# State-space heads: forward product and sum as one scalar_tensor_tensor per token tile

## The chip, the cores and the metric

The kernel runs on one core of one Trainium2 chip. The metric is the time of the program on the device in microseconds (us); less is better. The engines of the core run at once, each through its own queue in order: TensorE (PE for matmuls, PEld for the load of their stationary operand), VectorE (DVE), ScalarE (ACT), GpSimd (POOL) and SyncE (SP), which here only issues DMA transfers. They wait for each other by semaphores.

## The reference, cut to what matters

One inference step of a model of two layers, on 128 context tokens and 512 latent ones, all in fp32. Each layer has three branches read from one input projection, differential attention, a gated MLP, and a bidirectional state-space mixer with 16 heads. The mixer is the branch concerned:

```python
dt = jax.nn.softplus(dt_raw.reshape(bt, T, 2, M_HEADS).astype(F32) + dt_bias.astype(F32))
for d in range(2):                       # forward, backward
    dt_d = dt[:, :, d]
    y_d, fin = ssd_scan(_orient(xh * dt_d[..., None], d), _orient(dt_d * A[d], d),
                        _orient(bh, d), _orient(ch, d), init_states[:, d])
    ys.append(_orient(y_d, d) + d_skip[d].astype(F32)[:, None] * xh)
y = (ys[0] + ys[1]).reshape(bt, T, M_INNER)

# inside ssd_scan, chunks of 128 tokens:
a_cs = jnp.cumsum(a, -1)
decay_in = jnp.exp(segsum(a))
cb = jnp.einsum("bclhn,bcshn->bchls", c, b)
y_diag = jnp.einsum("bchls,bcshp->bclhp", cb * decay_in, xdt)
```

So inside each chunk a head needs a 128 x 128 matrix for each direction, c b^T under a triangular mask, times the step size dt of the source token and the decay between two tokens; it is multiplied with the head's values.

## The kernel before

**Data.** The 640 tokens are five tiles of 128. Weights stream from HBM in chunks of 128 x 1024. Every large matmul is done three times with operands split into a rounded high part and a rest: `w_hi` (L414, ScalarE) casts a chunk to its high part, `w_lo` (L423, VectorE) subtracts it to get the low part. `dense_F` (L535 to L537) then issues 24 matmuls per half of 320 tokens; one unit is 48 matmuls.

**Order.** One program order is written out by generators: TensorE's dense units are the clock (`tick`, after every six matmuls), and small tasks (`go`, with `yield n` for a pause of n ticks) put their instructions between. So the place of each instruction in its engine's queue is fixed when the program is built. Memory too is planned there: `Plan.place` runs the program once with nothing behind it, and lays each block (`al`, freed by `fr`) by first fit.

**The state-space stage.** For each pair of heads f (0 to 7 in the first layer; numbered on as 8 to 15 in the second) the units `xbc` and `z` run, after some of them (f = 3, 5, 7) also one of the gate projections `mga`. `ssd_pair` (L1334 to L1424) does what both heads share: the transposes of the values (L1343, copied by ScalarE at L1346), two products on GpSimd (L1354), the chunk states (matmuls L1365, recurrence L1373 on VectorE, copy of the final state L1376 on ScalarE, its store L1378 on the SP queue, copies L1382 and L1383), the output matmuls (L1394 with the head matrices M, L1396 with the states), their evacuation L1406, and the gate (L1412) and the sum of squares (L1420 on ScalarE, L1422) with products on GpSimd. Other tasks run between: the depthwise convolution (L1190 to L1194 copies, L1208 and L1214 on ScalarE, L1210, L1211 and L1216 on VectorE) and the gate of z (L1060 on ScalarE, L1062 on VectorE), and L1641, an evacuation with tanh on ScalarE.

**One head.** `ssd_head` (L1426) makes M for one head, 640 columns (five chunks of 128). `gf` and `gb` are c b^T under the two masks, shared by eight heads; `dt` has the step sizes, 32 columns (16 heads, two directions) for each of five tiles; `e[0]` and `e[1]` get the cumulated decay rows by DMA (L1437) and their bias by ScalarE (L1446, five instructions of 128 columns per direction). VectorE multiplies gf and gb by dt (L1443, once for each direction, two ticks apart), adds the two products (L1449), takes the smaller of the two exponents (L1451); ScalarE exponentiates (L1454), VectorE scales the states' operand (L1455) and forms M (L1457). The first head of a pair starts 5 ticks after its loads were issued and the second 12 (`D_HEAD`), so their instructions interleave.

Of the kernel before, what the change touches and what calls it, by code (L numbers as in the profile page):

```python
# [10 lines left out]
ALU = mybir.AluOpType  # L11
# [3 lines left out]
NT = 5  # L15
# [218 lines left out]
class Build:  # L234
# [1191 lines left out]
    def ssd_head(self, S, hh):  # L1426

        nc = self.nc
        f, l = S["f"], S["l"]
        h = 2 * f + hh  # L1430
        yield from self.until(lambda: f // 4 in self.G)
        gf, gb, cd = self.G[f // 4]
        e = [self.al(640) for _ in range(2)]
        ec = self.al(512)
        for d in range(2):
            j = 16 * d + h
            nc.sync.dma_start(out=self.v(e[d]), in_=self.csd[l][j:j + 1, :].to_broadcast([128, 640]))  # L1437
            nc.sync.dma_start(out=self.v(ec, 0, 512, 64 * d, 64 * d + 64), in_=self.ecd[l][j:j + 1, :].to_broadcast([64, 512]))
        yield D_HEAD[hh]
        d3 = self.v(self.dt).rearrange("p (c j) -> p c j", c=5)  # L1440
        w = [self.al(640) for _ in range(2)]
        for d, gg in enumerate((gf, gb)):
            nc.vector.tensor_tensor(out=self.v(w[d]).rearrange("p (c n) -> p c n", c=5), in0=self.v(gg).rearrange("p (c n) -> p c n", c=5),  # L1443
                                    in1=d3[:, :, 16 * d + h:16 * d + h + 1].to_broadcast([128, 5, 128]), op=ALU.mult)
            for c in range(NT):
                nc.scalar.activation(self.v(e[d], 128 * c, 128), self.v(e[d], 128 * c, 128), AF.Identity,  # L1446
                                     bias=self.v(self.cs, 32 * c + 16 * d + h, 1))
            yield 2
        nc.vector.tensor_tensor(out=self.v(w[0]), in0=self.v(w[0]), in1=self.v(w[1]), op=ALU.add)  # L1449

        nc.vector.tensor_tensor(out=self.v(e[0]), in0=self.v(e[0]), in1=self.v(e[1]), op=ALU.min)  # L1451
        self.fr(e[1], w[1])
        yield 2
        nc.scalar.activation(self.v(e[0]), self.v(e[0]), AF.Exp)  # L1454
        nc.vector.tensor_tensor(out=self.v(ec), in0=self.v(cd), in1=self.v(ec), op=ALU.mult)  # L1455
        yield 2
        nc.vector.tensor_tensor(out=self.v(e[0]), in0=self.v(e[0]), in1=self.v(w[0]), op=ALU.mult)  # L1457
        self.fr(w[0])
        S["M", hh], S["C", hh] = e[0], ec

    def ssd_end(self, l):
# [423 lines left out]
```

## Time and profile before

| | |
|---|---|
| time, median of 3 runs | 2187.92 us (2187.67 to 2189.08) |
| the profiled execution: time | 2191.47 us |
| its span (first to last instruction) | 2189.3 us |
| granted TensorE clock, mean | 0.996 |
| busy: PE, DVE, ACT, POOL | 98%, 66%, 47%, 8% |
| L1443, VectorE, 64 instructions | 0.81 us at least, 2.19 at most |
| L1449, VectorE, 32 instructions | 0.81 us at least, 1.94 at most |

The time of an execution is the span and about 2 us around it. Times inside the trace count from the start of the span. A line Lnnn is a line of the kernel before, also where the engine's work was issued by a helper. "Busy" of PE is not speed: matmuls are pipelined, and one of 320 columns is counted with 0.31 us while the next starts 0.14 us after it.

### The profile page before, as it was taken

How to read it: one execution, taken by the hardware profiler on the slowest of the kernel's cores; microseconds unless marked ns; L12 is line 12 of the kernel's file. 1: busy time of each engine (PE TensorE's matmuls, PEld its weight loads, DVE VectorE, ACT ScalarE, POOL GpSimd, SP SyncE). 2: the span in 40 equal slices, each digit the busy share in tenths (PEclk: the TensorE clock that was granted, in tenths of full speed). 3: DMA queues.
4: the chain of work that ended last, by engine and by line, in shares of the span. 5: the costliest groups of instructions: out<-in, count | busy, mean ns of one | idle time of the engine just before them, and what ended most of it. 6: DMA issues, size and time to landing. Idle time of an engine off the chain costs nothing.

```text
span 2189.3 us, 38380 instructions
## 1 busy us (share of the span) xinstructions
PE 2155.2 (98%) x15288; PEld 2090.4 (95%) x15288; DVE 1439.2 (66%) x2688; ACT 1032.8 (47%) x2240; POOL 184.0 (8%) x185
## 2 busy tenths in 40 slices
PE   7999999999999999999989999999999999999998
PEld 4999999999999999999879999999999999999996
DVE  5577677568556679976475777774464532799754
ACT  3566566532333257762265656563323322677521
POOL 0000000000101113320000000000001001132100
PEclk9999999999999999999999999999999999999999
DMA  7433333234224455633134333321222231555331
GB/s 295 123 102 99 90 102 104 85 120 145 77 78 147 166 153 155 165 95 135 68 121 119 100 91 101 110 77 63 94 77 69 78 119 41 141 155 147 117 125 49
DMA packets 94859, 246.17 MB, mean 112 GB/s; under 512 B 13940, under 2 KB 27348, under 8 KB 94680
## 3 DMA queue, kind: packets, MB, share of 16 engines
q1 hardware_dynamic: 94680, 243.72, 35.8%
q8 instruction: 120, 1.97, 0.4%
q14 instruction: 59, 0.48, 0.1%
HBM read 208.75 MB, written 8.70 MB: 99 GB/s over the span
## 4 chain that ended last, share of the span: by engine, by line
PE 88%; DVE 5%; ACT 3%; DMA 2%; issue 2%; SPq 0%; DVEq 0%; ACTq 0%
PE psum L536 19%; PE psum L537 19%; PE psum L535 18%; PE psum L477 6%; PE psum L476 6%; PE psum L478 6%; PE psum L964 4%; PE psum L1011 3%; PE psum L994 2%; DMA plain<-csd 1%; PE psum L1133 1%; DVE plain L1451 1%; DMA plain<-in_wp_dram 1%; PE psum L1394 1%; ACT rounded L414 1%
## 5 line engine op out<-in xcount | busy, mean ns | idle before, releaser
L536 PE MATMUL psum<-shared,rounded 128*128 128x320 f32 x3136 | 969.2, 309 | 0.0
L535 PE MATMUL psum<-shared,rounded 128*128 128x320 f32 x3136 | 967.0, 308 | 0.0
L537 PE MATMUL psum<-shared,rounded 128*128 128x320 f32 x3136 | 962.1, 307 | 0.0
L535 PEld LDWEIGHTS psum<-shared,rounded 128*128 128x128 f32 x3136 | 589.4, 188 | 4.5 <-issue 3.8
L537 PEld LDWEIGHTS psum<-shared,rounded 128*128 128x128 f32 x3136 | 589.3, 188 | 0.0
L536 PEld LDWEIGHTS psum<-shared,rounded 128*128 128x128 f32 x3136 | 587.8, 187 | 0.1
L423 DVE TENSOR_TENSOR rounded<-plain,rounded 128x1024 fp32r<-128x1024 f32 (+2 forms) x226 | 279.9, 1239 | 166.0 <-ACT rounded L414 159.7
L414 ACT CAST rounded<-plain 128x1024 fp32r<-128x1024 f32 (+2 forms) x226 | 235.3, 1042 | 188.7 <-PE psum L536 160.4
L476 PE MATMUL psum<-rounded,shared 128*128 128x256 f32 (+2 forms) x920 | 296.3, 322 | 0.0
L477 PE MATMUL psum<-rounded,shared 128*128 128x256 f32 (+2 forms) x920 | 292.2, 318 | 0.0
L478 PE MATMUL psum<-rounded,shared 128*128 128x256 f32 (+2 forms) x920 | 290.8, 316 | 0.9 <-DVE shared L850 0.9
L478 PEld LDWEIGHTS psum<-rounded,shared 128*128 128x128 f32 x920 | 173.7, 189 | 11.0 <-DVE shared L850 1.3
L476 PEld LDWEIGHTS psum<-rounded,shared 128*128 128x128 f32 x920 | 173.8, 189 | 8.7
L477 PEld LDWEIGHTS psum<-rounded,shared 128*128 128x128 f32 x920 | 173.7, 189 | 8.3 <-DVE rounded L423 0.2
L972 DVE TENSOR_REDUCE plain<-psum 128x1 f32<-128x640 f32 (+1 forms) x160 | 107.9, 714 | 88.0 <-PE psum L964 84.7
L978 ACT ACTIVATE plain<-psum,plain 128x640 f32<-128x640 f32 (+1 forms) x160 | 112.1, 709 | 4.5 <-DVE plain L972 3.0
L1641 ACT ACTIVATE plain<-psum 128x320 f32<-128x320 f32 x96 | 41.7, 437 | 129.8 <-PE psum L537 118.6
L964 PE MATMUL psum<-shared 128*128 128x320 f32 (+1 forms) x576 | 100.0, 312 | 0.1
L1707 POOL TENSOR_SCALAR plain<-plain 128x1024 f32<-128x1024 f32 x2 | 5.6, 2778 | 1003.9 <-DMA plain<-in_bs_dram 537.6
L1017 ACT ACTIVATE plain<-psum,plain 128x128 f32<-128x128 f32 x80 | 29.4, 368 | 124.3 <-PE psum L1011 85.3
L964 PEld LDWEIGHTS psum<-shared 128*128 128x128 f32 x576 | 84.6, 189 | 1.3 <-ACT plain L978 1.0
L1073 ACT ACTIVATE plain<-psum 128x320 f32<-128x320 f32 (+1 forms) x62 | 27.7, 447 | 121.0 <-PE psum L537 60.8
(277 smaller groups left out, 2687.6 us busy)
## 6 DMA issues: line engine op xcount, KB each, us to landing
plain<-in_wp_dram SPq DMA_DIRECT2D x252, 512.0 KB, 4.0
shared<-in_wp_dram SPq DMA_DIRECT2D x40, 512.0 KB, 7.2
shared<-csd SPq DMA_DIRECT2D x36, 320.0 KB, 5.8
shared<-shared SPq DMA_DIRECT2D x64, 160.0 KB, 3.0
plain<-csd SPq DMA_DIRECT2D x28, 320.0 KB, 5.3
plain<-plain SPq DMA_DIRECT2D x128, 64.0 KB, 2.0
plain<-in_wp_dram SPq DMA_DIRECT2D x12, 528.0 KB, 4.2
shared<-shared SPq DMA_DIRECT2D x32, 192.0 KB, 2.6
```

What stands on the lines that cost most here:

```text
L414: self.nc.scalar.copy(self.r(blk[0], 0, sz), self.v(self.w_raw[i], 0, sz))
L423: self.nc.vector.tensor_tensor(out=self.r(blk[1], 0, sz), in0=self.v(raw, 0, sz), in1=self.v(blk[0], 0, sz), op=ALU.subtract)
L476: mm(out, ht, wh, start=(k == 0), stop=False)
L477: mm(out, ht, wl, start=False, stop=False)
L478: mm(out, lt, wh, start=False, stop=(k == KD - 1))
L535: mm(out, wh, xh, start=(k == 0), stop=False)
L536: mm(out, wh, xl, start=False, stop=False)
L537: mm(out, wl, xh, start=False, stop=(k == KD - 1))
L964: mm(self.P[:, ss[m] + half, 0:n], self.r(H["q"], 1280 * i + 640 * m + 128 * t, 128), k, start=(i == 0), stop=(i == 1))
L972: nc.vector.tensor_reduce(out=self.v(st, m, 1), in_=src[m], op=ALU.max, axis=AX.XY if t else AX.X, negate=True)
L978: nc.scalar.activation(pv, src[m], AF.Exp, bias=self.v(st, m, 1), accum_out=self.v(st, 2 + m, 1))
L1011: mm(out, self.v(wt, 128 * j, 128), self.v(H["vg"], 256 * j + 256, 128) if j < 4 else self.v(H["cv"]), start=(j == 0), stop=(j == 4))
```

## The change

For each head the product of gf with the forward step sizes is no longer formed by itself. The backward product w = gb * dt stays one instruction and moves to the place where the forward one stood. At the place of the sum stand five instructions `scalar_tensor_tensor`, one for each token tile, w = gf * dt + w, where dt is a column of one number per partition. One block of 640 columns less is held per head, and the planner lays out the blocks anew.

```diff
         yield D_HEAD[hh]
         d3 = self.v(self.dt).rearrange("p (c j) -> p c j", c=5)
-        w = [self.al(640) for _ in range(2)]
-        for d, gg in enumerate((gf, gb)):
-            nc.vector.tensor_tensor(out=self.v(w[d]).rearrange("p (c n) -> p c n", c=5), in0=self.v(gg).rearrange("p (c n) -> p c n", c=5),
-                                    in1=d3[:, :, 16 * d + h:16 * d + h + 1].to_broadcast([128, 5, 128]), op=ALU.mult)
+        w = self.al(640)
+        nc.vector.tensor_tensor(out=self.v(w).rearrange("p (c n) -> p c n", c=5), in0=self.v(gb).rearrange("p (c n) -> p c n", c=5),
+                                in1=d3[:, :, 16 + h:17 + h].to_broadcast([128, 5, 128]), op=ALU.mult)
+        for d in range(2):
             for c in range(NT):
                 nc.scalar.activation(self.v(e[d], 128 * c, 128), self.v(e[d], 128 * c, 128), AF.Identity,
                                      bias=self.v(self.cs, 32 * c + 16 * d + h, 1))
             yield 2
-        nc.vector.tensor_tensor(out=self.v(w[0]), in0=self.v(w[0]), in1=self.v(w[1]), op=ALU.add)
+        for c in range(NT):
+            nc.vector.scalar_tensor_tensor(out=self.v(w, 128 * c, 128), in0=self.v(gf, 128 * c, 128), scalar=self.v(self.dt, 32 * c + h, 1),
+                                           in1=self.v(w, 128 * c, 128), op0=ALU.mult, op1=ALU.add)
 
         nc.vector.tensor_tensor(out=self.v(e[0]), in0=self.v(e[0]), in1=self.v(e[1]), op=ALU.min)
-        self.fr(e[1], w[1])
+        self.fr(e[1])
```

Below these lines w[0] is w. The changed kernel is two lines longer there: its L1442 is the backward product, L1450 the five new instructions, and its L1453, L1457 and L1459 are L1451, L1455 and L1457 of before.

On VectorE, in the first layer, at the pairs 2 and 3, before:

```order
879 L1406 SCALAR_TENSOR_TENSOR plain<-plain,psum 128x128
880 L1406 SCALAR_TENSOR_TENSOR plain<-plain,psum 128x512
881 L1449 TENSOR_TENSOR shared_7166<-shared_7166 128x640
882 L1451 TENSOR_TENSOR plain<-plain,shared_7166 128x640
883 L1455 TENSOR_TENSOR plain<-plain 128x512
884 L1062 SCALAR_TENSOR_TENSOR plain<-plain,psum 128x320
885 L1443 TENSOR_TENSOR shared_7166<-plain 128x640
886 L1457 TENSOR_TENSOR plain<-plain,shared_7166 128x640
887 L1443 TENSOR_TENSOR plain<-plain 128x640
888 L423 TENSOR_TENSOR rounded<-shared_7166,rounded 128x1024
889 L1373 SCALAR_TENSOR_TENSOR plain<-plain,psum 128x64 x6
890 L1449 TENSOR_TENSOR shared_7166<-shared_7166,plain 128x640
```

The first L1449 belongs to the first head of the pair, the two L1443 and the last L1449 to the second. At the same place in the changed kernel:

```order
876 L1406 SCALAR_TENSOR_TENSOR plain<-plain,psum 128x128
877 L1406 SCALAR_TENSOR_TENSOR plain<-plain,psum 128x512
878 L1450 SCALAR_TENSOR_TENSOR shared_7166<-plain,shared_7166 128x128 x5
879 L1453 TENSOR_TENSOR plain<-plain,shared_7166 128x640
880 L1457 TENSOR_TENSOR plain<-plain 128x512
881 L1062 SCALAR_TENSOR_TENSOR plain<-plain,psum 128x320
882 L1442 TENSOR_TENSOR shared_7166<-plain 128x640
883 L1459 TENSOR_TENSOR plain<-plain,shared_7166 128x640
884 L423 TENSOR_TENSOR rounded<-shared_7166,rounded 128x1024
885 L1373 SCALAR_TENSOR_TENSOR shared_7166<-shared_7166,plain,psum 128x64 x6
886 L1450 SCALAR_TENSOR_TENSOR shared_7166<-plain,shared_7166 128x128 x5
```

One L1443 of the two is gone, from between L1457 and L423, and each L1449 has become five instructions. On TensorE, ScalarE, GpSimd and the SP queue the instructions stand in the same order as before, only some tiles lie elsewhere.

## Rows read from the trace of the kernel before

**Rows 1.** The page, busy time, share of the span, instructions

```profile
PE 2155.2 (98%) x15288; PEld 2090.4 (95%) x15288; DVE 1439.2 (66%) x2688; ACT 1032.8 (47%) x2240; POOL 184.0 (8%) x185
```

**Rows 2.** Busy time by stage, 797 to 962 and 1876 to 2041 together

```profile
sum 330.00, PE 326.66 PEld 312.57 DVE 312.47 ACT 243.78 POOL 106.72; mean PE 163.33 PEld 156.29 DVE 156.23 ACT 121.89 POOL 53.36
```

**Rows 3.** Who waited for L1457: us in total, times

```profile
  PEld psum L1394: 5.8, 12
```

**Rows 4.** The chain of waits, pair 4 to 5: start, us, what

```profile
894.15 0.28 ACT plain L1376
894.44 0.34 SPq L1378
894.88 4.37 DMA shared<-csd
899.27 1.57 ACT shared L1446 x5
```

**Rows 5.** VectorE in order of time, pair 3: start, us, instruction, idle before

```profile
855.70 1.55 DVE L1443 TENSOR_TENSOR shared<-plain 128x640 f32<-128x640 f32 x2
...
858.13 1.23 DVE L423 TENSOR_TENSOR rounded<-shared,rounded 128x1024 fp32r<-128x1024 f32 x1 [0.48 <-ACT rounded L414]
859.27 1.00 DVE L1406 SCALAR_TENSOR_TENSOR plain<-plain,psum 128x128 f32<-128x128 f32 x2
860.19 0.82 DVE L1449 TENSOR_TENSOR shared<-shared 128x640 f32<-128x640 f32 x1
860.92 1.89 DVE L1451 TENSOR_TENSOR plain<-plain,shared 128x640 f32<-128x640 f32 x1
862.74 1.75 DVE L1455 TENSOR_TENSOR plain<-plain 128x512 f32<-128x512 f32 x1
864.41 0.47 DVE L1062 SCALAR_TENSOR_TENSOR plain<-plain,psum 128x320 f32<-128x320 f32 x1
864.81 1.54 DVE L1443 TENSOR_TENSOR shared<-plain 128x640 f32<-128x640 f32 x1
...
867.81 1.23 DVE L423 TENSOR_TENSOR rounded<-shared,rounded 128x1024 fp32r<-128x1024 f32 x1
```

**Rows 6.** GpSimd in order of time, pair 3

```profile
860.30 3.64 POOL L1354 TENSOR_TENSOR plain<-shared,plain 128x640 f32<-128x640 f32 x2 [9.80 <-ACT shared L1346]
863.90 1.76 POOL L1412 TENSOR_TENSOR plain<-plain 128x640 f32<-128x640 f32 x1
```

**Rows 7.** ScalarE in order of time, pair 3

```profile
862.85 0.74 ACT L1454 ACTIVATE plain<-plain 128x640 f32<-128x640 f32 x1 [2.36 <-DVE plain L1451]
863.49 3.02 ACT L1446 ACTIVATE shared<-shared,plain 128x128 f32<-128x128 f32 x10
...
866.74 1.04 ACT L414 CAST rounded<-shared 128x1024 fp32r<-128x1024 f32 x1
```

**Rows 8.** VectorE in order of time, attention end of the first layer

```profile
729.39 1.22 DVE L706 SCALAR_TENSOR_TENSOR plain<-plain 128x1024 f32<-128x1024 f32 x1
...
730.54 1.90 DVE L706 SCALAR_TENSOR_TENSOR plain<-plain 128x1024 f32<-128x1024 f32 x1
```

**Rows 9.** GpSimd at the same time

```profile
729.56 1.79 POOL L1165 TENSOR_TENSOR plain<-plain 128x320 f32<-128x320 f32 x1 [2.37 <-DVE plain L1162]
```

**Rows 10.** Groups by line and shape: count, busy us, mean ns

```profile
L820 DVE SCALAR_TENSOR_TENSOR shared<-plain,shared 128x128 fp32r<-128x128 f32 x8 | 2.8, 347 | 0.0
```

**Rows 11.** VectorE in order of time, pair 1

```profile
825.06 2.19 DVE L1457 TENSOR_TENSOR plain<-plain,shared 128x640 f32<-128x640 f32 x1
```

**Rows 12.** ScalarE in order of time, pair 4

```profile
880.15 0.44 ACT L1060 ACTIVATE plain<-psum 128x320 f32<-128x320 f32 x1 [0.67 <-PE psum L537]
```

**Rows 13.** VectorE in order of time, pair 4

```profile
882.94 1.94 DVE L1449 TENSOR_TENSOR shared<-shared 128x640 f32<-128x640 f32 x1
```

**Rows 14.** GpSimd in order of time, pair 4

```profile
882.25 1.95 POOL L1422 TENSOR_TENSOR plain<-plain,shared 128x640 f32<-128x640 f32 x1 [2.18 <-ACT shared L1420]
884.28 1.73 POOL L1354 TENSOR_TENSOR shared<-shared,plain 128x640 f32<-128x640 f32 x1
```

More of the change, by code (lines that the diff above doesn't have):

```diff
@@ L1456, in ssd_head @@
         yield 2
-        nc.vector.tensor_tensor(out=self.v(e[0]), in0=self.v(e[0]), in1=self.v(w[0]), op=ALU.mult)
-        self.fr(w[0])
+        nc.vector.tensor_tensor(out=self.v(e[0]), in0=self.v(e[0]), in1=self.v(w), op=ALU.mult)
+        self.fr(w)
         S["M", hh], S["C", hh] = e[0], ec
```

## The prediction

> **What bounds the kernel now.** The page comes first: TensorE is busy for 98% of the span, VectorE for 66% [rows 1]. A share over the whole span says little about an edit of one stage, so the second view is the table of stages. The state-space heads run in two stretches, one in each layer, at 797 to 962 and 1876 to 2041 us. In these 330 us TensorE is busy for 326.7 and VectorE for 312.5, which is 95%, with ScalarE at 74% [rows 2]. So both engines are nearly full there, and the question is which waits for which. The third view, who waited for line 1457, answers it: the matmuls of line 1394, which read the finished head matrix M, held their weight loads for it 12 times, 5.8 us together [rows 3]. The two stretches hold 16 pairs of heads; TensorE arrives a little before M in most of them. Nothing is to spare on the way to M.
>
> The fourth view, the chain of waits, shows that way closing on itself. DVE's L1373 of one pair releases L1376 on ScalarE, that the store L1378 on the SP queue; the loads of the next pair's decay rows (L1437) stand behind it in that queue, land 4.37 us later, and release ScalarE's L1446 [rows 4]. From there it goes through the weight split (L414 on ScalarE, L423 on VectorE) to L1449, L1451, the exponential L1454, ten L1446, the next L414 and L423, and to the next L1373. In pair 3 one sees each link [rows 5 to 7]: the first L423 starts at 858.13, L1451 begins at 860.92 and lasts 1.89, L1454 starts at 862.85 right behind it, ten L1446 and an evacuation follow, L414 starts at 866.74, and L423 at 867.81, where VectorE has just become free as well. A delay of L1451 is a delay of everything behind it, since ScalarE takes its instructions in order.
>
> **Why L1451 lasts 1.89 us.** The median of such an instruction, two SBUF operands of 640 columns, is 0.82; L1449 just before it shows that length [rows 5]. The difference is GpSimd. Its two products of L1354 start at 860.30 and are followed by L1412 at 863.90 [rows 6], and three VectorE instructions are long there: L1451 with 1.89, L1455 with 1.75, L1443 with 1.54. Each ends about 0.7 us after a GpSimd product does. L1062, which reads PSUM, starts inside the third product and takes 0.47 [rows 5]. So VectorE instructions with two SBUF operands and GpSimd products take turns, one instruction at a time, and a turn costs VectorE about 1.13 us: in pair 4 the product begun at 884.28 could not run until L1449 ended (882.94 + 1.94 = 884.88), and was over at 884.28 + 1.73 = 886.01 [rows 13, 14]. Scalar_tensor_tensor obeys as well: of two L706 back to back, a product of GpSimd that arrived in the first is let in before the second, which takes 1.90 instead of 1.22 [rows 8, 9].
>
> **The change part by part.** Per head, two instructions of 640 columns go: the forward product (L1443) and the sum (L1449). Five scalar_tensor_tensor of 128 columns come in the place of the sum; the backward product moves up to the place of the forward one. TensorE, ScalarE, GpSimd and the SP queue keep their order. Over 32 heads, 64 instructions go and 160 come.
>
> *Busy time of VectorE.* Neighbours overlap: two L1443 take 1.55 together [rows 5], so each occupies 1.55 - 0.82 = 0.73, and two that go free 1.47 us per head. The same form as the new one lasts 0.347 for 128 columns [rows 10]; with the same overlap of 0.09 it occupies 0.26, and five take 1.30. So VectorE is relieved by 0.17 us a head, 5.4 us in all. But the two halves lie in different places. The product that goes frees 0.73 before an L423 which waits for ScalarE anyway (in pair 3 VectorE idles 0.48 before the one at 858.13 [rows 5]), or before the second L423, where ScalarE's L414 is just as late (866.74 + 1.04 = 867.78 against 867.81 [rows 5, 7]). What hides the loss hides the gain: I count it as nothing. The sum that becomes five costs 1.30 - 0.73 = 0.57 more, in front of L1451, on the chain.
>
> *The turns.* Here is the larger term. In pair 3 the first GpSimd product arrives 0.11 us after L1449 began [rows 5, 6]. Now it waits for one piece of 0.26, runs 1.13, lets the second piece pass, and the next product is already due; after the third piece comes L1412. All three products fit between the five pieces: 0.34 + 1.13 + 0.2 + 1.13 + 0.2 + 1.13 + 0.2 + 0.26 + 0.75 for L1451 gives 5.3 to 5.4 us, where L1449 and L1451 took 2.62 (860.19 to 862.81). So L1451 ends about 2.8 us later: 0.57 for the pieces and 2.26 for two turns that used to fall behind it, on L1455 and L1443. Those two get shorter, but they are not on the chain. ScalarE's queue is: L1454, ten L1446 and L414 shift by 2.8, and with L414 the second L423 and L1373. The bounds are 0.57 (no more turns before L1451 than now) and 2.83 (two more); I take the upper, because every boundary between two such instructions in these rows is used by a product that waits.
>
> The Trainium skill weighs on the same side: SBUF — State Buffer, section "SBUF: two separate sides", says that the pair of ports which VectorE (with two SBUF inputs) and GpSimd share is locked for one whole instruction, and the other side blocks. By that rule five instructions offer five places to change over where one offered one, and the sum is the upper bound; if the five pieces held the ports as one, it would be the lower. L1451 and L706 agree with the rule at a boundary of two long instructions; no row here shows five short ones.
>
> *Pair by pair.* Three kinds. (a) Pairs 2, 3, 10 and 11, as worked out: 2.8 each to the chain. Pairs 1 and 9 are alike, but there VectorE is the later at the second L423, because L1457 was blocked for 2.19 [rows 11]; half, 1.4. Pair 0 and 8 start with slack: 0.2. (b) Pairs 4, 6, 12 and 14, before which one more unit of matmuls (a gate projection) stands: ScalarE waits for TensorE there (L1060, 0.67 [rows 12]), so the chain starts again from TensorE's own time, late by what TensorE is late. In pair 4, L1422 (882.25) already blocks L1449 (1.94 [rows 13, 14]); one turn moves, 1.13 + 0.57 less 0.2 for the L1443 that goes before it: 1.5. (c) Pairs 5, 7, 13 and 15 follow these: 2.65 to 2.85. The second head of a pair adds its own 0.57 behind L1373, not to the chain but to the M for which TensorE waits.
>
> First layer: 0.2 + 1.4 + 2.8 + 2.8 = 7.2 on the chain, 7.8 at TensorE after pair 3; pair 4 adds 1.5 + 0.57: 9.8 (chain 9.3); pair 5: 11.9 + 0.57 = 12.5; pair 6: 14.6 (chain 14.0); pair 7: 14.0 + 2.8 + 0.57 less 0.3 of slack = 17.1. Second layer the same less some 0.4 of slack in pair 9: 16.7. Together 33.8 us, nearly all of it as longer waits before L1394. The profiled execution took 2191.5, its span 2189.3; the median of the runs is 2187.9, 3.6 lower. The sum is a difference, so it is put on the median: 2187.9 + 33.8 = 2222.
>
> *Memory.* One block of 640 columns less per head lets the planner place other blocks elsewhere, and some loads wait for other predecessors. They are weight and state loads, which stand in the SP queue behind or before waits of ten microseconds and more; I count 0; one load of the chain missed would cost about a landing, 4.4 us [rows 4], to either side.
>
> **The rivals.** *No more turns* (20%). If GpSimd is not let in between pieces, or arrives after them, only 0.57 is left per pair on the chain and once more at its end: 0.57 x 3 + 0.57 = 2.3 after pair 3, then 0.9, 0.6, 0.9, 0.6: 5 per layer, 10 together, 2198. For it: no row shows short neighbours. Against it: rows 8 and 9. *VectorE was the bound and is relieved* (7%, the one that ends faster). Forward product and sum are long today where GpSimd blocks them; if the short pieces pass GpSimd's products without a turn, L1451 ends earlier than 2.6 us after the first piece begins, and the waits of rows 3 go: at most 5.8, 2182. Decided there: L1451 earlier than now after L1406. Against it: L706. *Slack takes it all* (7%): TensorE is late itself in pairs 4 to 7 and ScalarE is idle a quarter of the time [rows 2]; if the loads of the next pair were not tied to L1376, the delays would be made up: 2188. Against it: rows 4. *Worse than the sum* (6%): longer waits let TensorE's granted clock fall, or evacuations (L1062) come so late that banks are missing too; some 10 more, 2232.
>
> **How the numbers follow.** The forecast has 60%; its own range is 2212 to 2232 (a third of the moved turns missing, or the extra of the last case). The range of 80% reaches down to the case without more turns: 2196 to 2233. About 0.2%, 4.4 us, is what a measurement can tell here; faster than that 7%, within 8%, slower 85%.
>
> **What would show it.** In the changed profile: five pieces spread over more than 3 us, with GpSimd's products shorter (1.3 to 1.5 instead of 1.8); the successors of L1451 no longer blocked; ScalarE idle for about 5 us instead of 2.36 before L1454; waits of L1394 for M grown from 5.8 to nearly 40 us; other stages unchanged to 1 us. It would be wrong if the five pieces stand together in 1.4 us, or if L1394's waits do not grow.

## The result and the profile after

The changed kernel takes 2227.29 us (median of 4 runs, 2223.99 to 2229.77) against 2188.50 (2187.67 to 2189.99) for the kernel before in the same series: slower by 38.8 us, a ratio of 1.0176 with a 95% interval of 1.0163 to 1.0189. The forecast was 2222 in a range of 2196 to 2233. The profiled execution took 2229.77 us, its span 2227.8, which is 38.5 more than before.

Four line numbers to keep in mind: L1450 is the group of five new instructions, L1453 the minimum (L1451 before), L1456 the exponential (L1454 before) and L1459 the product that gives M (L1457 before).

First the row of the page with busy time, which answers to [rows 1]:

```profile
PE 2165.6 (97%) x15288; PEld 2099.6 (94%) x15288; DVE 1436.3 (64%) x2784; ACT 1033.0 (46%) x2240; POOL 168.4 (8%) x185
```

VectorE has 96 instructions more and is busy 2.9 us less. GpSimd runs the same 185 instructions in 15.6 us less. By this row alone the change looks like relief for both. The loss is in waiting, and it lies where the change lies. The table of stages has the two state-space stretches, now at 797 to 982 and 1896 to 2081 us (columns: stretch, its length, busy time of each engine with instructions, PEclk, DMA share, GB/s):

```profile
797.00:982.00 185.00, 171.78 (x1354) 163.71 (x1353) 156.49 (x264) 121.48 (x290) 46.90 (x51) 0.96 0.50 137
1896.00:2081.00 185.00, 167.09 (x1336) 159.35 (x1336) 153.75 (x262) 119.64 (x286) 44.52 (x50) 0.97 0.46 132
sum 370.00, PE 338.87 PEld 323.06 DVE 310.24 ACT 241.12 POOL 91.42; mean PE 169.43 PEld 161.53 DVE 155.12 ACT 120.56 POOL 45.71
```

Against [rows 2], VectorE, ScalarE and GpSimd do their work in less or the same busy time, in stretches 20 us longer each. TensorE was idle for 3.3 us of 330 and is now for 31.1 of 370. What it waits for is in the list of those that waited for line 1459 (us in total, times):

```profile
  PEld psum L1394: 34.5, 14
  PE psum L1394: 31.1, 13
```

The weight loads of L1394 waited 5.8 us for M in [rows 3] and wait 34.5 now. (The two rows are largely the same wait, seen by the load and by the matmul behind it, and are not added.) One link earlier on the chain, ScalarE's waits for the minimum, us in total, times and the longest, in the table of waits; before:

```profile
ACT plain L1454 <- DVE plain L1451: 20.9, 12, 2.4
ACT shared L1454 <- DVE shared L1451: 5.3, 4, 2.4
```

and after:

```profile
ACT plain L1456 <- DVE plain L1453: 50.1, 20, 5.0
ACT shared L1456 <- DVE shared L1453: 17.7, 10, 5.0
```

26.2 us have become 67.8. Pair 3 shows why, in the same view as [rows 5 to 7]. VectorE:

```profile
862.98 1.23 DVE L423 TENSOR_TENSOR rounded<-shared,rounded 128x1024 fp32r<-128x1024 f32 x1 [0.81 <-ACT rounded L414]
864.12 1.00 DVE L1406 SCALAR_TENSOR_TENSOR plain<-plain,psum 128x128 f32<-128x128 f32 x2
865.04 3.42 DVE L1450 SCALAR_TENSOR_TENSOR shared<-plain,shared 128x128 f32<-128x128 f32 x5
868.38 1.94 DVE L1453 TENSOR_TENSOR plain<-plain,shared 128x640 f32<-128x640 f32 x1
870.24 0.68 DVE L1457 TENSOR_TENSOR plain<-plain 128x512 f32<-128x512 f32 x1
870.85 0.47 DVE L1062 SCALAR_TENSOR_TENSOR plain<-plain,psum 128x320 f32<-128x320 f32 x1
871.24 0.81 DVE L1442 TENSOR_TENSOR plain<-plain 128x640 f32<-128x640 f32 x1
871.98 0.81 DVE L1459 TENSOR_TENSOR plain<-plain,shared 128x640 f32<-128x640 f32 x1
875.32 1.23 DVE L423 TENSOR_TENSOR rounded<-shared,rounded 128x1024 fp32r<-128x1024 f32 x1 [2.53 <-ACT rounded L414]
876.47 1.23 DVE L1373 SCALAR_TENSOR_TENSOR plain<-plain,psum 128x64 f32<-128x64 f32 x6
877.62 1.57 DVE L1450 SCALAR_TENSOR_TENSOR plain<-plain 128x128 f32<-128x128 f32 x5
```

GpSimd:

```profile
865.76 1.28 POOL L1354 TENSOR_TENSOR shared<-shared,plain 128x640 f32<-128x640 f32 x1 [10.51 <-ACT shared L1346]
867.00 1.31 POOL L1354 TENSOR_TENSOR plain<-shared,plain 128x640 f32<-128x640 f32 x1
868.27 1.37 POOL L1412 TENSOR_TENSOR plain<-plain 128x640 f32<-128x640 f32 x1
```

ScalarE:

```profile
870.36 0.74 ACT L1456 ACTIVATE plain<-plain 128x640 f32<-128x640 f32 x1 [4.10 <-DVE plain L1453]
871.00 3.03 ACT L1446 ACTIVATE shared<-shared,plain 128x128 f32<-128x128 f32 x10
...
874.25 1.04 ACT L414 CAST rounded<-shared 128x1024 fp32r<-128x1024 f32 x1
```

Read them side by side. The five pieces take 3.42 us here and 1.57 with the second head, where no product is due; alone they take 1.40 (the shortest of these groups). Two GpSimd products fell between them, and the third between the last piece and the minimum, which lasts 1.94 us (1.89 before, where it was the first product that came in; 0.81 undisturbed). So from the first piece to the end of the minimum it is 865.04 to 870.32, 5.28 us, where L1449 and L1451 took 2.62. The four that follow on VectorE are short now, and none is blocked; but the chain does not run through them. It runs through ScalarE, which waits: 4.10 us instead of 2.36 before the exponential, and its queue carries the delay to L414 and the second L423, before which VectorE idles 2.53 us. VectorE was held up, and then has nothing to do.

### The profile page after: what moved, and what is told of

It reads as the page before. It is cut to its first block, busy times and chain, and to the rows that moved or that the text cites. A ratio compares the mean times of both kernels' runs of the same rounds, so it can differ in the third digit from the quotient of the medians.

```text
span 2227.8 us, 38476 instructions
## 1 busy us (share of the span) xinstructions
PE 2165.6 (97%) x15288; PEld 2099.6 (94%) x15288; DVE 1436.3 (64%) x2784; ACT 1033.0 (46%) x2240; POOL 168.4 (8%) x185
## 5 line engine op out<-in xcount | busy, mean ns | idle before, releaser
L423 DVE TENSOR_TENSOR rounded<-plain,rounded 128x1024 fp32r<-128x1024 f32 (+1 forms) x225 | 278.6, 1239 | 169.9 <-ACT rounded L414 163.3
L414 ACT CAST rounded<-plain 128x1024 fp32r<-128x1024 f32 (+1 forms) x225 | 234.3, 1042 | 188.8 <-PE psum L536 165.7
L1643 ACT ACTIVATE plain<-psum 128x320 f32<-128x320 f32 x96 | 41.7, 437 | 131.4 <-PE psum L537 120.9
L1073 ACT ACTIVATE plain<-psum 128x320 f32<-128x320 f32 (+1 forms) x62 | 27.7, 447 | 121.0 <-PE psum L537 60.8
L423 DVE TENSOR_TENSOR rounded<-shared,rounded 128x1024 fp32r<-128x1024 f32 x37 | 45.3, 1226 | 58.0 <-ACT rounded L414 58.0
```

What stands on the lines that cost most here:

```text
L414: self.nc.scalar.copy(self.r(blk[0], 0, sz), self.v(self.w_raw[i], 0, sz))
L423: self.nc.vector.tensor_tensor(out=self.r(blk[1], 0, sz), in0=self.v(raw, 0, sz), in1=self.v(blk[0], 0, sz), op=ALU.subtract)
L1643: nc.scalar.activation(self.half_of(tm, half), self.P[:, b, 0:320], AF.Tanh, scale=0.5)
```

## The experiments

All times are medians with the ratio to the kernel before, run on the same chip in the same series (2188.5 to 2188.9 there).

### One piece in place of five

The theory is that the number of instructions counts, not what they compute. This kernel is the changed one with the five instructions as one of 640 columns.

```diff
-        for c in range(NT):
-            nc.vector.scalar_tensor_tensor(out=self.v(w, 128 * c, 128), in0=self.v(gf, 128 * c, 128), scalar=self.v(self.dt, 32 * c + h, 1),
-                                           in1=self.v(w, 128 * c, 128), op0=ALU.mult, op1=ALU.add)
+        nc.vector.scalar_tensor_tensor(out=self.v(w), in0=self.v(gf), scalar=self.v(self.dt, h, 1),
+                                       in1=self.v(w), op0=ALU.mult, op1=ALU.add)
```

> The changed kernel with the five scalar_tensor_tensor replaced by one of 640 columns, which takes the step sizes of the first token tile for all five (the result of M is other; everything else is as in the change, the placement of blocks too). Theory of turns: one instruction gives one place to change over, as L1449 did; it occupies 0.74 to 0.80 instead of 0.73, so 2186 to 2192, no measurable difference from before. Rival (fusion, pointer scalar, moved product or placement costs): 2205 to 2227.

Measured: 2187.63 us, ratio 0.9998 (0.9989 to 1.0007). The whole loss is gone. With it go three other suspects that this kernel shares with the changed one: the missing forward product, the moved backward product, and a block of memory less per head. VectorE in pair 3 (here L1449 is the one piece, L1452 the minimum and L1456 the scaling of the states' operand):

```profile
858.34 0.88 DVE L1449 SCALAR_TENSOR_TENSOR shared<-plain,shared 128x640 f32<-128x640 f32 x1
859.13 1.90 DVE L1452 TENSOR_TENSOR plain<-plain,shared 128x640 f32<-128x640 f32 x1
860.95 1.75 DVE L1456 TENSOR_TENSOR plain<-plain 128x512 f32<-128x512 f32 x1
```

One turn before the end of the minimum, as in [rows 5]. It also says what the instruction itself is worth: to fuse a product into the sum, one instruction of 640 columns fewer per head, gains nothing that can be measured.

### The sum in five pieces, nothing else

The other half of the test: the kernel before, with both products kept, and only the sum split.

```diff
-        nc.vector.tensor_tensor(out=self.v(w[0]), in0=self.v(w[0]), in1=self.v(w[1]), op=ALU.add)
+        for c in range(NT):
+            nc.vector.tensor_tensor(out=self.v(w[0], 128 * c, 128), in0=self.v(w[0], 128 * c, 128), in1=self.v(w[1], 128 * c, 128), op=ALU.add)
```

> The kernel before, with only the sum (L1449) issued as five tensor_tensor of 128 columns; both products stay, nothing is fused or moved. Theory of turns (five short instructions in front of L1451 let all three GpSimd products in, and L1451 delays ScalarE's chain): most of the change's loss comes back, since the pieces alone make the turns. A piece of 128 columns without a pointer scalar should occupy about 0.2 us, so five cost 1.0 to 1.1 against 0.73, some 0.25 less per head than the change: 2215 to 2225. Rival (the fused operation with its pointer scalar, the product that moved, or the new placement of blocks is what costs): the sum in pieces changes nothing of these, so 2188 to 2194.

Measured: 2216.02 us, ratio 1.0128 (1.0114 to 1.0142). Splitting alone costs 27.4 us, with a plain addition and no scalar operand. In pair 2 all three products come in between the pieces, in pair 3 none does (here L1450 is a piece, L1452 the minimum):

```profile
836.31 4.40 DVE L1450 TENSOR_TENSOR shared<-shared 128x128 f32<-128x128 f32 x5
840.64 0.81 DVE L1452 TENSOR_TENSOR plain<-plain,shared 128x640 f32<-128x640 f32 x1
...
858.87 1.10 DVE L1450 TENSOR_TENSOR shared<-shared 128x128 f32<-128x128 f32 x5
859.88 0.81 DVE L1452 TENSOR_TENSOR plain<-plain,shared 128x640 f32<-128x640 f32 x1
```

4.40 less 1.10 is 3.30, three turns of 1.10. In pair 3 the first L1354 started at 860.12, after the pieces were through; these five are shorter than the five of the change (1.10 against 1.40), so some pairs slip past (1, 3, 9 and 11). That is one reason why it costs less than the change. There is another, which limits the theory. In pair 1 the first L1354 started ahead of the last piece, and still it was not let in at once. GpSimd, then VectorE behind the pieces (816.28 to 817.37):

```profile
816.90 2.94 POOL L1354 TENSOR_TENSOR plain<-shared,plain 128x640 f32<-128x640 f32 x1 [14.12 <-ACT shared L1346]
817.29 0.82 DVE L1452 TENSOR_TENSOR plain<-plain,shared 128x640 f32<-128x640 f32 x1
818.03 0.68 DVE L1456 TENSOR_TENSOR plain<-plain 128x512 f32<-128x512 f32 x1
```

The last piece, the minimum and L1456 all passed it at their undisturbed length. Of the 62 products of L1354, L1412 and L1422 here, 6 were passed in this way, all of L1354; of those in the change 2, in pairs 0 and 8. Why these were not let in is open.

### The sum in two pieces

The same with 384 and 256 columns.

```diff
+        for o, n in ((0, 384), (384, 256)):
+            nc.vector.tensor_tensor(out=self.v(w[0], o, n), in0=self.v(w[0], o, n), in1=self.v(w[1], o, n), op=ALU.add)
```

> The kernel before with the sum in two tensor_tensor of 384 and 256 columns. Theory of turns: one more place to change over in front of the minimum, so one turn of 1.13 moves there instead of two, and 0.07 for the second instruction: about 0.1 + 0.6 + 1.2 + 1.2 on the chain of the first pairs and 1.2 for each later one, 8 us per layer: 2200 to 2208, between before and e1. Rival (loss grows with the number of instructions only, five give 27.5): a quarter of that, 2193 to 2197.

Measured: 2203.31 us, ratio 1.0066 (1.0051 to 1.0081). VectorE in pair 3, the two pieces and the minimum:

```profile
858.87 1.96 DVE L1450 TENSOR_TENSOR shared<-shared 128x384 f32<-128x384 f32 x2
860.75 1.88 DVE L1452 TENSOR_TENSOR plain<-plain,shared 128x640 f32<-128x640 f32 x1
```

They take 0.89 us undisturbed (in the second head of the pair), so they hold one turn, and the minimum holds the next: two before the exponential where the kernel before has one. One boundary more costs 14.8 us over both layers, four boundaries more cost 27.4. The number of turns does not explain that difference: up to the end of the minimum, the rows of the 16 first heads show 16 turns before, 29 with two pieces and 30 with five (three each in ten pairs, none in six). The five are longer by 0.21 us per head (1.10 against 0.89), 3.4 us over the first heads. And after their three turns TensorE waits longest, 3.9 and 4.3 us for M in pairs 2 and 10; around these waits its granted clock is 0.50 for 6.8 us each (852.2 to 859.0 and 1944.5 to 1951.3 us). With two pieces it falls once, for 3.4 us (853.4 to 856.8). At half speed this is up to 5.1 us of the difference, an estimate; the rest is open.

### The minimum ahead of the pieces

If the turns cost time only because they stand in front of ScalarE's exponential, then they should be harmless behind the minimum. The changed kernel, its minimum taken first (it needs nothing of the sum):

```diff
+        nc.vector.tensor_tensor(out=self.v(e[0]), in0=self.v(e[0]), in1=self.v(e[1]), op=ALU.min)
         for c in range(NT):
             ...
-        nc.vector.tensor_tensor(out=self.v(e[0]), in0=self.v(e[0]), in1=self.v(e[1]), op=ALU.min)
```

> The changed kernel with the minimum (L1451 of before) issued ahead of the five pieces instead of behind them; results are the same. Theory of the chain (the loss comes because the minimum, and with it ScalarE's exponential and the next weight cast, waits behind the turns): the minimum is early, ScalarE runs ahead, and what is left is VectorE's own queue, with three turns and 0.57 us of pieces in it, about 0.5 us later at the second L423 and 0.6 more at M: 2190 to 2200. Rival (the turns cost by VectorE's busy time, wherever they lie): the same turns are taken, so 2220 to 2230.

Measured: 2190.29 us, ratio 1.0007 (0.9998 to 1.0017). One line moved takes back 37 of the 38.8 us. VectorE in pair 3 (L1449 the minimum, L1451 the pieces):

```profile
858.12 0.82 DVE L1449 TENSOR_TENSOR plain<-plain,shared 128x640 f32<-128x640 f32 x1
858.85 3.44 DVE L1451 SCALAR_TENSOR_TENSOR shared<-plain,shared 128x128 f32<-128x128 f32 x5
862.21 1.81 DVE L1456 TENSOR_TENSOR plain<-plain 128x512 f32<-128x512 f32 x1
```

and GpSimd:

```profile
859.59 1.27 POOL L1354 TENSOR_TENSOR shared<-shared,plain 128x640 f32<-128x640 f32 x1 [14.47 <-DMA shared<-in_wp_dram]
860.82 1.32 POOL L1354 TENSOR_TENSOR plain<-shared,plain 128x640 f32<-128x640 f32 x1
862.10 1.37 POOL L1412 TENSOR_TENSOR plain<-plain 128x640 f32<-128x640 f32 x1
```

The turns are all there, two in the pieces (3.44) and one behind. They are simply in no one's way. So neither the pieces themselves nor VectorE's work as such makes the loss; the place of the turns does.

### The same reordering in the kernel before

If that frees ScalarE by one turn per pair, the kernel before should gain from it.

```diff
-        nc.vector.tensor_tensor(out=self.v(w[0]), in0=self.v(w[0]), in1=self.v(w[1]), op=ALU.add)
         nc.vector.tensor_tensor(out=self.v(e[0]), in0=self.v(e[0]), in1=self.v(e[1]), op=ALU.min)
+        nc.vector.tensor_tensor(out=self.v(w[0]), in0=self.v(w[0]), in1=self.v(w[1]), op=ALU.add)
```

> The kernel before with the minimum ahead of the sum; nothing else. Theory of the chain: the minimum ends 1.8 us earlier, ScalarE with it. In pairs where VectorE waits for ScalarE at the second L423 (0.7 us in the pairs with a gate projection) this comes off the chain, elsewhere VectorE's queue is as late, so 2182 to 2188, at the edge of what is measurable. Rival (VectorE's queue alone sets the pace): 2188, no difference.

Measured: 2193.72 us, ratio 1.0026 (1.0015 to 1.0036). A miss: slower by 5.1 us. GpSimd and VectorE in pair 3 (L1449 the minimum, L1456 the product that gives M):

```profile
868.27 1.59 POOL L1422 TENSOR_TENSOR plain<-plain,shared 128x640 f32<-128x640 f32 x1 [1.01 <-ACT shared L1420]
```

```profile
867.87 0.81 DVE L1456 TENSOR_TENSOR plain<-plain,shared 128x640 f32<-128x640 f32 x1
868.60 1.94 DVE L1443 TENSOR_TENSOR shared<-plain 128x640 f32<-128x640 f32 x1
870.47 1.21 DVE L423 TENSOR_TENSOR rounded<-shared,rounded 128x1024 fp32r<-128x1024 f32 x1
```

ScalarE, one turn earlier, squares y earlier (L1420), and so GpSimd's L1422 comes earlier. In the kernel before it started at 868.49 in this pair, while VectorE was in the second L423, and ran beside L1373, which reads PSUM. Now it starts 0.3 us ahead of the last product L1443, which then lasts 1.94 and stands before the second L423. The turn that was taken off the chain at one place came back at another.

### That kernel without L1422

To test this explanation, the last kernel with L1422 left out.

```diff
-            nc.gpsimd.tensor_tensor(out=self.v(self.acc), in0=self.v(self.acc), in1=self.v(sq), op=ALU.add)
```

> The kernel before with the minimum ahead of the sum, as in e4, and without GpSimd's L1422 (left out: the sum of squares over the head pairs). Since e4 made ScalarE earlier, L1422 came earlier too and blocked the L1443 in front of the second L423 (2.19 instead of 0.82), where before it fell beside L1373, which reads PSUM. Theory: without L1422 that turn is gone and the early minimum shows: 2182 to 2188. Rival (the order itself costs, not the turn): 2192 to 2195 as e4.

Measured: 2185.42 us, ratio 0.9983 (0.9974 to 0.9992). The 8.3 us between the two kernels are what those 14 additions cost on GpSimd there, though GpSimd is idle for over nine tenths of the time. Not all of it need be the turn itself. In the profile with L1422, TensorE waits 2.6 and 2.4 us for M in pairs 2 and 10, and behind that its granted clock is 0.50 (857.2 to 860.5 and 1939.2 to 1942.5 us); without L1422 it is 1.00 in both stages.

### Without two of GpSimd's products

The price of the five pieces by themselves: the changed kernel and the kernel before, both without GpSimd's products L1354 and L1412. (L1422 stays, and takes one turn with the pieces or the sum in pairs 4, 6, 12 and 14 of both.)

```diff
-            nc.gpsimd.tensor_tensor(
-                ...
-            xds.append(xd)
+        xds = [xt, xt]
...
-        nc.gpsimd.tensor_tensor(out=self.v(y), in0=self.v(y), in1=self.v(S["z"]), op=ALU.mult)
```

The changed kernel without them:

> The changed kernel without GpSimd's products L1354 and L1412 (left out: the scaling of the values for the chunk states, and the gate of y; the values and y are used as they are). With e6 as its partner it shows what the five pieces cost where nothing takes turns with them. Theory of turns: the pieces alone are 0.57 us per head, and without turns the chain has 2 to 3 us per pair to spare, so 2180 to 2187, within 3 us of e6. Rival (pieces, fusion or the moved product cost by themselves): at least 10 us above e6.

The kernel before without them:

> The kernel before without the same two products of GpSimd (same parts left out). Theory of turns: nothing blocks VectorE three times per pair, so the waits of the output matmuls for M (5.8 us in the kernel before) go: 2180 to 2187. Rival (GpSimd costs VectorE nothing there): 2187 to 2190.

Measured: 2184.94 us (ratio 0.9984, 0.9975 to 0.9994) and 2179.35 us (0.9961, 0.9947 to 0.9976). A partial miss: the two were to lie within 3 us and lie 5.6 apart, and the second is 0.65 us below its range. So without these products the pieces cost 5.6 us, and of the change's 38.8 us some 33 need the products. It also shows how little there was to win: with no turns by these products at all, the kernel before is only 9 us faster.

### A version to beat both

By the theory the kernel with the minimum first lacks only a better place for L1422. So L1422 goes to VectorE, late enough to stand among the products of the next pair, in front of an L423 that VectorE waits for. Once with the minimum first, once without it.

```diff
-            yield 3
-            nc.gpsimd.tensor_tensor(out=self.v(self.acc), in0=self.v(self.acc), in1=self.v(sq), op=ALU.add)
+            yield (8 if f in (1, 6) else 15) if f < 7 else 3
+            nc.vector.tensor_tensor(out=self.v(self.acc), in0=self.v(self.acc), in1=self.v(sq), op=ALU.add)
```

With the minimum first:

> The kernel before with the smaller exponent taken ahead of the sum of the two products, and the accumulation of the squares of y (L1422) moved from GpSimd to VectorE, where it is issued so late that it stands among the products of the next pair, ahead of a first L423 that VectorE waits for. All of the result is computed. Theory of turns: no GpSimd instruction is left that can fall in front of the second L423, so what the early minimum cost before (2193.7) goes; from the 2185.4 of the same kernel without L1422, and up to 1 us for 14 more VectorE instructions of 0.73 that stand before waits: 2183 to 2188, the same as the kernel before or up to 0.2% faster. Rival (VectorE at 95% in this stage is a bound by its work alone): 14 instructions of 0.73 add 10 us to it, of which at least half shows: 2190 to 2196.

With the order of the kernel before:

> The kernel before with L1422 alone moved to VectorE in the same way, the order of sum and minimum as in the kernel before. All of the result is computed. Theory of turns: one GpSimd product less per pair; where L1422 blocked L1449 or L1451 (pairs 4 to 7, 1.13 us each) the chain gains, less than 0.7 each for the instruction that VectorE has now: 2182 to 2188. Rival (VectorE's work alone is the bound): 2192 to 2198.

Measured: 2189.78 us (ratio 1.0006, 0.9997 to 1.0015) and 2188.23 us (0.9997, 0.9988 to 1.0006). Neither beats the kernel before. Both are misses: the first lies above its range by 1.8 us (and just below the rival's), the second by 0.2. The trace shows the waits as intended: in the kernel with the order of before, those who waited for L1457 are

```profile
  PEld psum L1394: 3.7, 4
  PE psum L1394: 2.7, 2
```

where the weight loads waited 5.8 us before [rows 3]. The medians do not show these 2.1 us. The profiled execution of that kernel, its fastest (2185.89 us), has them: from the first L1394 of pair 0 to the last of pair 15 it is 813.6 to 2036.4 us, and 816.8 to 2041.7 before, 2.1 us less. Against runs that spread from 2185.89 to 2191.12 a gain of this size is not shown.

## Why the prediction was right, and where its sizes were off

**The mechanism.** It is the one forecast: GpSimd's products take their turns at the boundaries between the short pieces, in front of the minimum, and ScalarE's queue carries the delay to the next pair. The pair of experiments on the number of pieces and the one with the minimum first show it from three sides: without the boundaries no loss, with the boundaries alone most of it, with the boundaries off the chain none. The time from the first piece (or the sum) to the end of the minimum, summed over the 16 first heads, goes with the loss: against the kernel before it is 2.0 us longer with one piece, 15.0 with two, 20.3 with the sum in five and 35.1 in the change, and the kernels take 0.95 us less, 14.8, 27.4 and 38.8 more. The rule cited from the Trainium skill (SBUF — State Buffer, section "SBUF: two separate sides"), by which the shared ports are held for one whole instruction, is borne out for short neighbours as well, which no row before showed: a product that waits is let in after a single piece, and L1354 and L1412 then show 1.27 to 1.46 us. That every boundary is used, which the prediction took from its rows, is not so: the split sum shows products that were passed. And one link of the chain is not confirmed. ScalarE's L1446 waited for the loads of the decay rows, the link of [rows 4], 8.0 us in ten waits before, and waits 2.4 us in seven now. No run tests how much of the delay is handed on over the store and the loads.

**The size of a turn.** Forecast 1.13, measured 1.10 in the split sum (4.40 against 1.10, three turns) and 1.03 to 1.04 in the pieces of the change (4.48 to 4.53 against 1.40; once 4.79, which gives 1.13). From first piece to the end of the minimum: forecast 5.3 to 5.4, measured 5.28 in pair 3.

**Pair by pair.** The start of the first L1394 that needs M of the second head, after minus before, from the timeline of TensorE, with what was there already at the first pair of the layer taken off (-0.95 at pair 0, 17.50 at pair 8). The -0.95 is older than the stage and fits TensorE's granted clock, which is 0.50 from 27.7 to 34.5 us before and from 28.5 to 31.8 after. The forecast's first two numbers are worked out from its terms (0.2 + 1.4 + 0.57, and 2.8 more); from pair 9 on it is 0.4 less in layer 2:

| pairs | forecast at TensorE | layer 1 | layer 2 |
|---|---|---|---|
| 1, 9 | 2.2 | 3.5 | 3.1 |
| 2, 10 | 5.0 | 6.2 | 6.3 |
| 3, 11 | 7.8 | 9.2 | 8.9 |
| 4, 12 | 9.8 | 11.1 | 11.0 |
| 5, 13 | 12.5 | 12.3 | 13.5 |
| 6, 14 | 14.6 | 13.9 | 16.9 |
| 7, 15 | 17.1 (16.7 in layer 2) | 16.4 | 19.6 |
| to the end of the stage | as above | 18.4 | 20.9 |

The last row is the first pair of layer 2 for layer 1 (17.50 + 0.95), and the last L1394 for layer 2 (2041.7 before and 2080.1 after, 38.4 less 17.5). Together 39.4, less 0.95 from the start, is the difference of the spans to 0.1 us; forecast were 33.8. The sum fell short by 5 us. That layer 1 agrees at pair 7 (16.4 against 17.1) is luck, since pairs 1 and 5 were off in opposite directions. The terms that were mis-sized are these.

*Pairs 1 and 9* were given half, 1.4 each, because VectorE was the later engine there. They took the full length: 3.5 and 3.1 at TensorE against 2.2. Their L1449 and L1451 held no turn before; now the rows of these pairs hold three. Pair 9:

```profile
1916.82 4.53 DVE L1450 SCALAR_TENSOR_TENSOR shared<-plain,shared 128x128 f32<-128x128 f32 x5
1921.27 0.81 DVE L1453 TENSOR_TENSOR plain<-plain,shared 128x640 f32<-128x640 f32 x1
```

*Pair 5* was too high: only two of three products came in time there, the third (916.87) ran behind the minimum. In pair 13, its twin, all three came in, as the rows of both show (pair 5 first):

```profile
913.37 2.41 DVE L1450 SCALAR_TENSOR_TENSOR shared<-plain,shared 128x128 f32<-128x128 f32 x5
915.71 1.89 DVE L1453 TENSOR_TENSOR shared<-shared 128x640 f32<-128x640 f32 x1
...
2010.96 4.48 DVE L1450 SCALAR_TENSOR_TENSOR shared<-plain,shared 128x128 f32<-128x128 f32 x5
2015.37 0.81 DVE L1453 TENSOR_TENSOR plain<-plain,shared 128x640 f32<-128x640 f32 x1
```

*The clock* stood among the rivals, as part of the case worse than the sum. It happened. The table of stretches around the last wait of pair 7 (PEclk is the third number from the end):

```profile
973.60:976.40 2.80, 0.82 (x6) 0.38 (x4) 2.54 (x6) 2.15 (x6) 0.00 (x0) 1.00 0.66 202
977.30:980.70 3.40, 3.40 (x30) 3.07 (x27) 2.06 (x3) 0.06 (x1) 0.00 (x0) 0.51 0.72 251
980.80:984.00 3.20, 3.20 (x24) 3.20 (x24) 0.16 (x1) 0.44 (x1) 1.56 (x1) 1.00 0.01 5
```

TensorE stood still for some two us; in the stretch behind it the granted clock is 0.51, the lower of its two levels (1.2 GHz), and TensorE is busy for all of it; then 1.00 again. Such a stretch, 3.4 us at half speed, costs up to 1.7 us, an estimate. It lies behind pair 7 and pair 15, where the table above grows by 2.0 and 1.3 us after the last pair. There are seven in the two stages after the change and none before, so at most 12 us in all. What the other five cost is not told apart, since TensorE waits for M soon after them anyway.

**The pieces** were counted with 0.57 us per head on the chain, 10 us in all if nothing else happened (the rival without more turns). The size per head is right (a first head without turns takes 2.13 us from the first piece to the end of the minimum, against 1.55). The pair of kernels without those products shows 5.6 in all, so what hangs on the products, some 33 us, was forecast too low. Counting the rows of the first heads before and after, 25 turns more fall in front of the minimum (16 before, 41 after), where the working had 20 and, for pairs 1 and 9, half a price. At 1.03 to 1.10 us that is 26 to 28 us. How the rest divides between TensorE's clock and the length of the pieces is open.

**VectorE's relief** of 0.17 us per head was counted as nothing. It is there in busy time (2.9 us less in the whole span). One piece in place of five relieves VectorE by more, and gains 0.95 us, not told apart from zero. **Memory**, counted 0, is in that kernel too, and shows no effect.

**The signs named in advance.** The pieces spread over 3.42 us (over 3 was forecast); GpSimd's products 1.28 to 1.37 us (1.3 to 1.5); nothing blocked behind the minimum; the waits of L1394 34.5 us (nearly 40). ScalarE's idle time was 4.10 instead of about 5: its last work before the wait, the evacuation L1643, ended 3.28 us after the first L423 began (866.26 against 862.98), where it was 2.36 before, and so 0.9 us of the delay is not idle time. In the stretch 0 to 797 us TensorE is busy for 781.42 us before and 781.19 after, in the 885 us between the two stages (985 to 1870, and 1004 to 1889 after) 877.90 and 877.79: outside the two stages nothing moved.

**The rivals.** Slack that takes it all and a relieved VectorE are out by the result. No more turns is out by the rows of pair 3.

## What to carry to other kernels

Where VectorE and GpSimd both work on SBUF, count the boundaries between VectorE's instructions with two SBUF operands on the chain to the next engine, not their busy time: each is a place where a waiting GpSimd product can come in, at 1.03 to 1.13 us here. If short instructions must be, put them behind whatever another engine waits for; here one line moved was worth 37 us. And before a turn is moved off the chain, look where it lands: an engine that is let go earlier sends its own followers earlier too.

## What the runs showed of the hardware

- A GpSimd product that waits is mostly let in at the first boundary between two VectorE instructions, even where the next one is ready and only 128 columns long. Three products went through five pieces of 1.10 us together and made them 4.40. Not always: in the split sum 6 of 62 products were passed by VectorE instructions with two SBUF operands, and one of them lasted 2.94 us.
- GpSimd's products show 1.27 to 1.46 us where they take turns with pieces, and L1354 shows 1.70 to 1.91 in the kernel before, beside long instructions (such as [rows 6, 14]). Its busy time fell from 184.0 to 168.4 us for the same work. So busy time of GpSimd in a profile is not its work alone.
- In the change, waits of TensorE's weight loads for M of 2.0 to 4.6 us were followed by 3.4 us of granted clock near 0.5 seven times; other waits, of up to 3.1 us, were not.
- The split into two costs half of the split into five (14.8 and 27.4 us) with nearly as many turns (29 and 30): three turns in one pair make TensorE wait longer, and its clock falls for longer (6.8 us twice, against 3.4 once).
